# Norm 2 and the last step with a PSUM buffer per token tile, late-split columns, column sums by transposes, and buffers at multiples of 64 bytes

## The chip, the cores and the metric

The kernel runs on one core of a Trainium2 chip. The metric is device time in microseconds (us) of one execution; the median of several runs is quoted, and beside it one execution was recorded by the hardware profiler. Engines are named as the profile names them: PE is the matmul engine (TensorE), PEld its weight load, DVE is VectorE, ACT is ScalarE, POOL is GpSimd and SP is SyncE, which here issues nearly all transfers.

## The reference, cut to what matters

One layer of a diffusion backbone in fp32: 256 latent tokens of width 2048 (`x`), 256 context tokens, one conditioning vector `c` that yields six modulation vectors.

```python
mod = silu(c) @ w_mod + b_mod                      # (6 * 2048): sh1 sc1 g1 sh2 sc2 g2, segments 0 to 5
hx  = modulate(rms_norm(x, norm1_g), sh1, sc1)     # modulate(h, s, c) = h * (1 + c) + s
out = token_mixer(hx, ...)                         # two branches, gated and merged, then merged @ w_o
x   = x + g1 * out
h2  = modulate(rms_norm(x, norm2_g), sh2, sc2)     # "norm 2"
a, b = split(h2 @ w_up)                            # w_up: 2048 x 11264
a   = dwconv_grid(a, ffn_dw) + ffn_db              # 3 x 3 on a 4 x 64 grid
x   = x + g2 * ((silu(a) * b) @ w_down)            # w_down: 5632 x 2048
return rms_norm(x, final_g)
```

The change touches the segments 2 to 5 of `mod`, `merged @ w_o` with norm 2 behind it, the first columns of `h2 @ w_up`, and `@ w_down` with the last norm.

## The kernel before

**Products.** Every fp32 operand is split in two: a high half `hi` that is rounded to fp32r (ScalarE copy, L116) and a low half `lo`, the difference (VectorE subtraction, L117). A product is hi*hi + lo*hi + hi*lo. Weights come in blocks of 1 MB (`wload`, issued from SP, L78) into four buffers `raw`, and are split in halves of 1024 columns by `wsplit`: `w_hi` has five buffers, and the low halves lie first in the pool `lop` (five buffers on the right side of the memory), later in a ring `lo_ring` of one buffer `w_lo` (L659) and parts of the big activation tile `H` that are free by then (L634, L762), which is why a low half appears in the profile as `H`. The list `behind_of` says for the next splits on which engine the subtraction runs and after which instruction it is queued.

**Column blocks (`proj`).** The output is feature-major: 256 columns of a weight are two PSUM banks (a "bank pair", L57; three pairs exist). For each block of 8 k (k is a group of 128 rows), 16 wide matmuls of 128x512 take the high half of the weight times both halves of the activation, and 16 narrow ones of 128x256 the low half; `wide_next` swaps which of the two comes first from one block to the next. All matmuls are recorded at L135.

**Token products (`token_product`, `residual`).** `merged @ w_o` and `@ w_down` are token-major: four column blocks `cq` of 512, and for each two token tiles t of 128 tokens, six matmuls of 128x512 per k. `residual` multiplies by the broadcast gate `macc` (L830), adds to `x` (L831), sums squares on ScalarE (L833) and, at cq = 3, takes root (L837) and reciprocal (L838). At cq = 3 the second token tile is cut in two pieces of 256 columns (`pieces`) for every k, and the first piece shares a bank pair with token tile 0.

**Modulation beside the main work (`mod_steps`).** `pump` takes one step at a time, put between the other products: VectorE accumulates `silu(c)` times a row block of `w_mod` into `macc` (128 x 2048, cleared by a memset on POOL, L665, with the bias row behind it in POOL's queue). Segments 4 and 3, in this order, need their sum over the partitions as columns: `pc` (L672 to L679), 16 matmuls of one column with `macc` as weights. Segments 2 and 5 become rows broadcast to all partitions.

**Norm 2.** `x` is transposed by PE (`ptx`, L871), scaled by `g2c` into `xg`; the two reciprocals go on diagonals `dg` (L864, one buffer), whose product with ones, `rb`, spreads them over the partitions. Then a loop over eight pairs of k multiplies `xg` by `rb` (L886), adds `sh2` and rounds on ScalarE (the high half of h2) and subtracts on VectorE (L891, the low half); VectorE's order is written by hand there (`manual_schedule`). The first block of w_up follows with `proj` on two column blocks. Elsewhere a scheduler, which works from a model of the times, orders each engine's instructions.

**The end.** After cq = 3 of w_down the last norm scales `x` (ScalarE and VectorE) and SP issues eight stores (L970), four for each token tile.

Of the kernel before, what the change touches and what calls it, by code (L numbers as in the profile page):

```python
# [16 lines left out]
P = 128  # L17
T = 256
# [18 lines left out]
def hybrid_layer_kernel(ctx: ExitStack, tc: tile.TileContext, I, out, dbg=None):  # L37
# [19 lines left out]
    def bank_pair(name):  # L57

        return psW.tile([P, 2, 512], F32, name=name, tag="acw")
# [337 lines left out]
    def proj(w, cols, src, kt):  # L397
# [16 lines left out]
                wide_next[0] = not wide_next[0]  # L414
        return [acc[:].rearrange("p n (s t) -> p n s t", s=2) for acc in accs]

    def proj_xc(w, cols):
# [244 lines left out]
    def mod_steps():  # L662
        for seg in (4, 3, 2, 5):
            acc = map_.tile([P, D], F32, name="macc", tag="macc")
            nc.gpsimd.memset(acc[:], 0.0)  # L665
            nc.gpsimd.dma_start(acc[0:1, :], b_mod[0:1, seg * D:seg * D + D])
            for k in range(KD):
                raw = wload([(w_mod[k * P:k * P + P, seg * D:seg * D + D], (2048,))])
                nc.vector.scalar_tensor_tensor(out=acc[:], in0=raw[:], scalar=cst[:, k, 0:1], in1=acc[:], op0=ALU.mult, op1=ALU.add)  # L669
                if k < KD - 1:  # L670
                    yield
            if seg in (3, 4):  # L672
                pc = psH.tile([P, KD], F32, name="pc2", tag="psh")
                for k in range(KD):
                    mm(pc[:, k:k + 1], acc[:, k * P:k * P + P], ones[:, 0:1], k == 0, k == KD - 1)
                if seg == 3:
                    nc.vector.tensor_copy(sh2[:], pc[:])
                else:
                    nc.vector.scalar_tensor_tensor(out=g2c[:], in0=pc[:], scalar=1.0, in1=n2g, op0=ALU.add, op1=ALU.mult)  # L679
# [100 lines left out]
    def token_product(w, kt, cq, part, tail=1):  # L780


        accs = {}
        slots = [bank_pair("to")] + ([bank_pair("to")] if cq == 3 else [])
        slots = [pair[:, i] for pair in slots for i in range(2)]
        for t in range(2):
            for i, cs in enumerate(pieces(cq, t)):
                accs[t, i] = slots[t + i][:, :cs.stop - cs.start]

        def product(t, i, k, src, hv, lv):  # L790
            ts = slice(t * P, t * P + P)
            cs = pieces(cq, t)[i]
            mm(accs[t, i], src(k % 2, 0)[:, ts], hv[:, cs], k == 0, False)
            mm(accs[t, i], src(k % 2, 0)[:, ts], lv[:, cs], False, False)
            mm(accs[t, i], src(k % 2, 1)[:, ts], hv[:, cs], False, k == kt - 1)

        todo = []
        for c in range(kt // 4):
            for k4, hv, lv in wviews([wblock(w, c * 512, 4, cq * 512, 512)], 4):
                k = 4 * c + k4  # L800
                if k % 2 == 0:
                    src = part(k)
                todo.append((k, src, hv, lv))
            if c < kt // 4 - tail:
                for args in todo:
                    for t, i in accs:
                        product(t, i, *args)
                todo = []
        for t in range(2):
            own = range(len(pieces(cq, t)))  # L810
            for args in todo[:-4]:
                for i in own:
                    product(t, i, *args)
            for i in own:
                for args in todo[-4:]:
                    product(t, i, *args)
        return accs

    def pieces(cq, t):

        return (slice(0, 256), slice(256, 512)) if cq == 3 and t == 1 else (slice(0, 512),)

    def residual(accs, cq, bc, pool):

        for t in range(2):
            for i, cs in enumerate(pieces(cq, t)):
                n = cs.stop - cs.start
                xs = slice(cq * 512 + cs.start, cq * 512 + cs.stop)
                tt = pool.tile([P, 512], F32, name="res", tag="res", bufs=1)
                nc.vector.tensor_tensor(out=tt[:, :n], in0=accs[t, i], in1=bc[:, xs], op=ALU.mult)  # L830
                nc.vector.tensor_tensor(out=x1[:, t, xs], in0=x1[:, t, xs], in1=tt[:, :n], op=ALU.add)  # L831
                sq = pool.tile([P, 512], F32, name="sq", tag="sq", bufs=1)
                nc.scalar.activation(sq[:, :n], x1[:, t, xs], AF.Square, accum_out=ssq2[:, cq + i, t:t + 1])  # L833
            if cq == 3:
                if t == 1:
                    nc.vector.scalar_tensor_tensor(out=ssq2[:, 0, 1:2], in0=ssq2[:, 3, 1:2], scalar=1.0 / D, in1=ssq2[:, 0, 1:2], op0=ALU.mult, op1=ALU.add)
                root = nc.scalar.activation(r2[:, t:t + 1], ssq2[:, 3 + t, t:t + 1], AF.Sqrt, scale=1.0 / D, bias=ssq2[:, 0, t:t + 1])  # L837
                nc.vector.reciprocal(r2[:, t:t + 1], r2[:, t:t + 1])  # L838
        if cq in (1, 2):
            nc.vector.tensor_tensor(out=ssq2[:, 0, :], in0=ssq2[:, 0, :], in1=ssq2[:, cq, :], op=ALU.add)  # L840
        if cq == 2:
            nc.vector.tensor_scalar(out=ssq2[:, 0, :], in0=ssq2[:, 0, :], scalar1=1.0 / D, scalar2=EPS, op0=ALU.mult, op1=ALU.add)
        return root if cq == 3 else None

    def mg_part(k0):
        return lambda k, p: mg[:, k0 + k, p, :]
# [10 lines left out]
    for cq in range(4):  # L857
        accs = token_product(w_o, KD, cq, mg_part)
        norm2 = residual(accs, cq, bcast[2], tw)
        if cq == 3:  # L860
            rb = bank_pair("rb")[:, 0, 0:T]
            for t in range(2):
                dg = tw.tile([P, P], F32, name="dg", tag="dg", bufs=1)
                nc.vector.tensor_scalar(out=dg[:], in0=ident[:], scalar1=r2[:, t:t + 1], scalar2=None, op0=ALU.mult)  # L864
                mm(rb[:, t * P:t * P + P], ones, dg[:], t == 0, t == 1)
        for k2 in range(2):
# [13 lines left out]
    h2_hi = {}  # L880
    h2_lo = {}
    with tc.manual_schedule(engines={nc.vector.engine}):
        for k2 in range(KD // 2 + 1):
            if k2 < KD // 2:
                ks = slice(2 * k2, 2 * k2 + 2)
                nc.vector.tensor_tensor(out=xg[:, ks, :], in0=xg[:, ks, :], in1=rbv, op=ALU.mult)  # L886
                for k in range(2 * k2, 2 * k2 + 2):
                    h2_hi[k2] = nc.scalar.activation(hx[:, k, 1, :], xg[:, k, :], AF.Identity, bias=sh2[:, k:k + 1])
            if k2 > 0:
                for k in range(2 * k2 - 2, 2 * k2):  # L890
                    h2_lo[k2 - 1] = nc.vector.scalar_tensor_tensor(out=hx[:, k, 0, :], in0=xg[:, k, :], scalar=sh2[:, k:k + 1], in1=hx[:, k, 1, :].bitcast(F32),  # L891
                                                   op0=ALU.add, op1=ALU.subtract)
# [12 lines left out]
    w_up = I["w_up"][0]  # L905
    for j in range(NF // 2):
        cols = [256 * j, FF + 256 * j]
        pa_, pb_ = proj(w_up, cols, hx, KD) if j == 0 else proj(w_up, cols[:1], hx, KD) + [None]
# [51 lines left out]
    for t in range(2):  # L960
        for cq in (0, 1, 3, 2):
# [8 lines left out]
            nc.sync.dma_start(out[0, t * P:t * P + P, cs], v1)  # L970


_INS = ["x", "c", "ctx", "c_ctx", "w_mod", "b_mod", "norm1_g", "w_in", "lb_raw", "a_norm_g", "sconv_w",
# [29 lines left out]
```

## Time and profile before

| | |
|---|---|
| median of 3 runs | 1745.35 us (1743.7 to 1745.82) |
| profiled execution | 1744.56 us, its span 1742.6 us |
| PE busy | 1706.6 us, 98% of the span |
| VectorE, ScalarE, POOL busy | 76%, 52%, 1% |
| mean granted TensorE clock | 0.991 |
| DMA | 384.85 MB, mean 221 GB/s |

The span is the time from the first to the last recorded work of the profiled execution; 1.96 us of its 1744.56 lie around it. A row of a timeline gives start and length in us, the engine, the line, the operation, out<-in and shapes; in brackets stands the idle time of the engine just before, and what ended it. "128*128 128x512" is a weight tile of 128 by 128 with 512 columns that stream by. The granted clock (PEclk) is a share of full speed. In a row of groups stand the line, operation and shapes, then busy time and mean ns of one, then the idle time before.

### The profile page before, as it was taken

Reading aid. Unit: us, or ns where it says so; the run is one execution under the profiler, and the core shown is the slowest. Engines: PE = TensorE matmul, PEld = TensorE weight load, DVE = VectorE, ACT = ScalarE, POOL = GpSimd, SP = SyncE. Lnnn points to the kernel's source line nnn. Section 1 sums busy time; section 2 is a strip of 40 time slices with the busy share of each in tenths; the row PEclk is TensorE's granted clock in tenths of the full one; section 3 lists DMA queues with packets and bytes.
Section 4 is the critical chain, followed back from the end, with each engine's and each line's share of the span. In section 5 each row is a group of like instructions: output and inputs, shape, how many; then the busy total and the mean of one; then the engine's idle time right before and its main releaser. Section 6 shows DMA issues by size and latency. Waiting matters only on the chain.

```text
span 1742.6 us, 24110 instructions
## 1 busy us (share of the span) xinstructions
PE 1706.6 (98%) x9623; PEld 1443.0 (83%) x9623; DVE 1316.2 (76%) x1694; ACT 899.7 (52%) x1156; POOL 20.0 (1%) x25
## 2 busy tenths in 40 slices
PE   5999999999999999999999899999999999999997
PEld 3567878788888888898888788888888888888886
DVE  4447267668998978878865589888888877876774
ACT  5226246556655644544555454444555554765653
POOL 0000000000000000000000100000000000000000
PEclk9999999999999999999999899999999999999999
DMA  9996323224777778878976357776666755655552
GB/s 360 348 336 196 105 64 121 73 97 148 263 248 265 270 252 312 311 285 325 328 273 205 116 198 242 242 242 236 233 236 238 241 173 190 218 193 193 194 193 73
DMA packets 293045, 384.85 MB, mean 221 GB/s; under 512 B 7780, under 2 KB 245645, under 8 KB 284102
## 3 DMA queue, kind: packets, MB, share of 16 engines
q1 hardware_dynamic: 291968, 379.82, 63.7%
q10 hardware_dynamic: 694, 3.24, 0.5%
q8 instruction: 75, 1.23, 0.3%
q0 software_dynamic: 272, 0.26, 0.1%
q14 instruction: 36, 0.29, 0.1%
HBM read 381.20 MB, written 2.10 MB: 220 GB/s over the span
## 4 chain that ended last, share of the span: by engine, by line
PE 97%; DVE 1%; ACT 1%; issue 0%; DMA 0%; ACTq 0%; DVEq 0%
PE acc L135 56%; PE to L135 19%; PE acx L135 6%; PE vacc L135 5%; PE zacc L135 5%; PE pm L135 2%; PE ps L135 2%; PE po L135 1%; PE pc L135 0%; DMA rows_a<-in_norm_g_dram 0%; PE pt L247 0%; PE pm L324 0%; PE kdt L510 0%; ACT H L233 0%; DVE xt L240 0%
## 5 line engine op out<-in xcount | busy, mean ns | idle before, releaser
L116 ACT ACTIVATE w_hi<-raw 128x1024 fp32r<-128x1024 f32 x506 | 533.3, 1058 | 463.7 <-PE acc L135 334.3
L135 PE MATMUL acc<-H,w_hi 128*128 128x512 f32 x2688 | 636.6, 392 | 2.9 <-DVE H L891 2.3
L117 DVE TENSOR_TENSOR H<-raw,w_hi 128x1024 fp32r<-128x1024 f32 x427 | 517.9, 1221 | 133.1 <-ACT w_hi L116 124.4
L135 PEld LDWEIGHTS acc<-H,w_hi 128*128 128x128 f32 x2688 | 500.5, 189 | 104.3 <-DVE H L891 3.3
L135 PEld LDWEIGHTS acc<-H 128*128 128x128 f32 x2360 | 297.3, 192 | 7.4 <-DVE H L117 1.1
L135 PE MATMUL acc<-H 128*128 128x256 f32 x2360 | 303.1, 284 | 0.1
L135 PE MATMUL to<-w_hi,H 128*128 128x512 f32 (+1 forms) x792 | 221.4, 365 | 0.0
L669 DVE SCALAR_TENSOR_TENSOR macc<-raw,cst,macc 128x2048 f32<-128x2048 f32 x64 | 150.3, 2348 | 27.9 <-DMA raw<-in_w_mod_dram 24.0
L135 PEld LDWEIGHTS to<-w_hi,H 128*128 128x128 f32 x792 | 142.8, 188 | 24.3
L135 PE MATMUL to<-H 128*128 128x512 f32 (+1 forms) x396 | 144.9, 366 | 0.0
L117 DVE TENSOR_TENSOR w_lo<-raw,w_hi 128x1024 fp32r<-128x1024 f32 x78 | 94.8, 1221 | 62.0 <-ACT w_hi L116 53.3
L926 DVE SCALAR_TENSOR_TENSOR cvf<-av,pf,cvf 128x189 f32<-128x189 f32 (+2 forms) x352 | 130.3, 425 | 0.7 <-ACT cvf L914 0.7
L131 ACT ACTIVATE H<-y 128x512 fp32r<-128x512 f32 x88 | 55.1, 630 | 87.8 <-PE to L135 86.2
L135 PE MATMUL acx<-H,w_hi 128*128 128x512 f32 x288 | 93.3, 398 | 0.0
L132 DVE TENSOR_TENSOR H<-y,H 128x512 fp32r<-128x512 f32 x88 | 60.6, 690 | 36.8 <-ACT H L131 36.6
L135 PEld LDWEIGHTS to<-H 128*128 128x128 f32 x396 | 74.6, 188 | 12.2
L135 PE MATMUL vacc<-w_hi,H 128*128 128x512 f32 x256 | 82.2, 398 | 0.0
L135 PE MATMUL to<-w_hi,mg 128*128 128x512 f32 (+1 forms) x288 | 81.1, 367 | 0.0
L135 PE MATMUL zacc<-H,w_hi 128*128 128x512 f32 x224 | 78.1, 412 | 1.9 <-ACT H L335 1.9
L135 PEld LDWEIGHTS acx<-H,w_hi 128*128 128x128 f32 x288 | 53.6, 188 | 12.5
L135 PEld LDWEIGHTS zacc<-H,w_hi 128*128 128x128 f32 x224 | 42.0, 190 | 26.0 <-issue 10.9
L335 ACT ACTIVATE H<-xsT,md 128x256 fp32r<-128x256 f32 x32 | 16.7, 591 | 84.9 <-DVE md L329 84.9
(229 smaller groups left out, 1579.0 us busy)
## 6 DMA issues: line engine op xcount, KB each, us to landing
raw<-in_w_up_dram SPq DMA_DIRECT2D x88, 1024.0 KB, 4.9
raw<-in_w_in_dram SPq DMA_DIRECT2D x81, 1024.0 KB, 5.1
raw<-in_w_mod_dram SPq DMA_DIRECT2D x64, 1024.0 KB, 5.1
raw<-in_w_down_dram SPq DMA_DIRECT2D x44, 1024.0 KB, 5.0
raw<-in_w_mod_dram SPq DMA_DIRECT2D x64, 512.0 KB, 6.8
raw<-in_w_o_dram SPq DMA_DIRECT2D x16, 1024.0 KB, 5.0
raw<-in_w_in_dram SPq DMA_DIRECT2D x16, 512.0 KB, 3.8
raw<-in_w_pa_dram SPq DMA_DIRECT2D x8, 1024.0 KB, 5.3
```

The costliest lines, as they stand in the source:

```text
L116: nc.scalar.activation(hi, half, AF.Copy)
L117: sub.tensor_tensor(op=ALU.subtract, **operands)
L131: nc.scalar.activation(hi, src, AF.Copy)
L132: nc.vector.tensor_tensor(out=lo, in0=src, in1=hi.bitcast(F32), op=ALU.subtract)
L135: return nc.tensor.matmul(o, lhsT, rhs, start=start, stop=stop, skip_group_check=True)
L335: upper = nc.scalar.activation(H[:, kk, 1 + i, :], src, AF.Identity, scale=mv[:, 1, k, i:i + 1], bias=mv[:, 0, k, i:i + 1])
L669: nc.vector.scalar_tensor_tensor(out=acc[:], in0=raw[:], scalar=cst[:, k, 0:1], in1=acc[:], op0=ALU.mult, op1=ALU.add)
L926: nc.vector.scalar_tensor_tensor(out=c4[:, ro, co], in0=a4[:, ri, ci], scalar=pf[:, tap * NF + f:tap * NF + f + 1], in1=c4[:, ro, co], op0 ...
```

## The change

Eight edits, with L-numbers of before:

1. A tile of 32 bytes (`edge`) is put at the right edge of the memory, so that the pools on the right side (`lop`, `map`, `tp`, `xp`: w_lo, macc, z, x1 and others) begin at multiples of 64 bytes; before, they began 32 bytes off one.
2. Column sums of segments 4 and 3: 16 transposes by PE in four groups of 4, each group summed along its free axis by a TENSOR_REDUCE on VectorE.
3. `token_product` at cq = 3: a bank pair for each token tile, and a third bank (`rest`) for the last four k of the right 256 columns of tile 1; only these four k are cut in pieces of 256. `residual` does the 512 columns of tile 1 first, then `rest`. Root and reciprocal of tile 0 are queued ahead of the work on tile 1.
4. Two buffers for `dg`.
5. The first multiply of the h2 loop is cut in two of 256 columns, and the first pair of low halves comes ahead of the second multiply.
6. The first block of w_up goes by `proj_both`: both column blocks per 8 k, all wide matmuls ahead of all narrow ones.
7. The subtractions around the loop: the first three are free to run ahead of it, all on VectorE (before, one, on POOL); of those tied to the loop five are left. The memset of `macc` for segment 5 is queued after the last low half of h2.
8. The last of the eight stores is issued by ScalarE.

```diff
+    edge = ctx.enter_context(tc.tile_pool(name="edge", bufs=1, side="right"))
+    edge.tile([P, 8], F32, name="edge")
     lop_cm = tc.tile_pool(name="lop", bufs=5, side="right")
...
+    def proj_both(w, cols, src):
+        accs = [bank_pair("acc") for _ in cols]
+        for c in range(KD // 8):
+            both = zip(*[wsplit([wblock(w, c * 1024, 8, c0, 256)]) for c0 in cols])
+            parts = [(8 * c + 4 * i + k, k * 256, part) for i, part in enumerate(both) for k in range(4)]
+            for wide in (True, False):
+                for k, at, part in parts:
+                    for acc, p in zip(accs, part):
...
+        wide_next[0] = False
...
+                if seg == 5:
+                    behind.enter_context(tc.issue_after(h2_lo[KD // 2 - 1].ins))
+                nc.gpsimd.memset(acc[:], 0.0)
...
-                pc = psH.tile([P, KD], F32, name="pc2", tag="psh")
-                for k in range(KD):
-                    mm(pc[:, k:k + 1], acc[:, k * P:k * P + P], ones[:, 0:1], k == 0, k == KD - 1)
...
+                for k4 in range(KD // 4):
+                    pc = psH.tile([P, 4, P], F32, name="pc", tag="psh")
+                    for k in range(4):
+                        at = (4 * k4 + k) * P
+                        nc.tensor.transpose(pc[:, k, :], acc[:, at:at + P], ident[:])
+                    nc.vector.tensor_reduce(out=col[:, 4 * k4:4 * k4 + 4], in_=pc[:], op=ALU.add, axis=mybir.AxisListType.X)
...
+            accs = [bank_pair("to")[:, 0] for t in range(2)]
+            rest = bank_pair("to")[:, 0, 0:256]
...
+                for args in todo[-4:]:
+                    product(t, *args, cs=slice(0, 256))
+                for args in todo[-4:]:
+                    product(t, *args, acc=rest, cs=slice(256, 512))
...
-                dg = tw.tile([P, P], F32, name="dg", tag="dg", bufs=1)
+                dg = tw.tile([P, P], F32, name="dg", tag=f"dg{t}", bufs=1)
...
-    behind_of += [((), nc.gpsimd)] + [((h2_hi[i], h2_lo[i]), nc.vector) for i in range(7)]
+    behind_of += [((), nc.vector)] * 3 + [((h2_hi[i], h2_lo[i]), nc.vector) for i in (1, 3, 4, 5, 6)]
...
-            nc.sync.dma_start(out[0, t * P:t * P + P, cs], v1)
+            (nc.scalar if t == 1 and cq == 2 else nc.sync).dma_start(out[0, t * P:t * P + P, cs], v1)
```

How the instructions stand on PE around the first column sum (`pc`; `acc` are the column blocks of `proj`, `pt<-ident,rows_f` are transposes of the convolution's weights), before:

```order
L135 MATMUL acc<-H 128x256 x32
L135 MATMUL acc<-H,w_hi 128x512 x16
L135 MATMUL pc_4931<-ones_r,macc 128x1 x16
L135 MATMUL acc<-H,w_hi 128x512 x16
L135 MATMUL acc<-H,w_lo 128x256 x8
L740 MATMUL pt<-ident,rows_f 128x110 x3
L135 MATMUL acc<-H 128x256 x3
```

And after:

```order
L137 MATMUL acc<-H,w_hi 128x512 x16
L700 MATMUL pc<-ident,macc 128x128 x8
L137 MATMUL acc<-H,w_hi 128x512 x16
L137 MATMUL acc<-H,w_lo 128x256 x5
L700 MATMUL pc<-ident,macc 128x128 x4
L137 MATMUL acc<-H,w_lo 128x256 x2
L700 MATMUL pc<-ident,macc 128x128 x4
L137 MATMUL acc<-H,w_lo 128x256
L137 MATMUL acc<-H 128x256 x24
L137 MATMUL acc<-H,w_hi 128x512
L764 MATMUL pt<-ident,rows_f 128x110 x3
```

The 16 one-column matmuls in one place became 16 transposes in groups of 8, 4 and 4, with matmuls of the main work between them.

VectorE from the last products of w_o to the first pairs of h2 (`res` and `x` are the residual, `r` the reciprocal, `xg` the multiply by `rb`, `H<-xg,sh,H` the low halves of h2, `H<-raw,w_hi` low halves of weights), before:

```order
L117 TENSOR_TENSOR H<-raw,w_hi 128x2x512
L830 TENSOR_TENSOR res<-to,macc 128x512
L831 TENSOR_TENSOR x_7188<-x_7188,res 128x512
L830 TENSOR_TENSOR res<-to,macc 128x256
L831 TENSOR_TENSOR x_7188<-x_7188,res 128x256
L830 TENSOR_TENSOR res<-to,macc 128x256
L838 RECIPROCAL r_7190<-r_7190 128x1
L836 SCALAR_TENSOR_TENSOR ssq_7189<-ssq_7189 128x1
L831 TENSOR_TENSOR x_7188<-x_7188,res 128x256
L864 TENSOR_SCALAR dg<-ident,r_7190 128x128
L838 RECIPROCAL r_7190<-r_7190 128x1
L864 TENSOR_SCALAR dg<-ident,r_7190 128x128
```

And after:

```order
L119 TENSOR_TENSOR H<-raw,w_hi 128x2x512 x4
L853 TENSOR_TENSOR res<-to,macc 128x512
L854 TENSOR_TENSOR x_7205<-x_7205,res 128x512
L853 TENSOR_TENSOR res<-to,macc 128x512
L854 TENSOR_TENSOR x_7205<-x_7205,res 128x512
L863 RECIPROCAL r_7207<-r_7207 128x1
L853 TENSOR_TENSOR res<-to,macc 128x256
L907 TENSOR_SCALAR dg<-ident,r_7207 128x128
L883 SCALAR_TENSOR_TENSOR ssq_7206<-ssq_7206 128x1
L854 TENSOR_TENSOR x_7205<-x_7205,res 128x256
L863 RECIPROCAL r_7207<-r_7207 128x1
L907 TENSOR_SCALAR dg<-ident,r_7207 128x128
```

Four weight subtractions now stand right ahead of the first residual, where one stood, and the residual of tile 1 covers 512 columns and then 256.

VectorE in the h2 loop behind that, before:

```order
L886 TENSOR_TENSOR xg<-xg,rb 128x512 x2
L891 SCALAR_TENSOR_TENSOR H<-xg,sh_3465,H 128x256 x2
L886 TENSOR_TENSOR xg<-xg,rb 128x512
L117 TENSOR_TENSOR H<-raw,w_hi 128x2x512
L891 SCALAR_TENSOR_TENSOR H<-xg,sh_3465,H 128x256 x2
```

And after:

```order
L930 TENSOR_TENSOR xg<-xg,rb 128x256 x2
L938 SCALAR_TENSOR_TENSOR H<-xg,sh_3469,H 128x256 x2
L932 TENSOR_TENSOR xg<-xg,rb 128x512 x2
L938 SCALAR_TENSOR_TENSOR H<-xg,sh_3469,H 128x256 x2
L932 TENSOR_TENSOR xg<-xg,rb 128x512
L119 TENSOR_TENSOR H<-raw,w_hi 128x2x512
```

The second multiply moved behind the first low halves, and the first subtraction inside the loop one pair later.

More of the change, by code (lines that the diff above doesn't have):

```diff
@@ L664, in mod_steps @@
             acc = map_.tile([P, D], F32, name="macc", tag="macc")
-            nc.gpsimd.memset(acc[:], 0.0)
+            with ExitStack() as behind:
+                if seg == 5:
+                    behind.enter_context(tc.issue_after(h2_lo[KD // 2 - 1].ins))
+                nc.gpsimd.memset(acc[:], 0.0)
             nc.gpsimd.dma_start(acc[0:1, :], b_mod[0:1, seg * D:seg * D + D])
@@ L780, in token_product, with product @@
     def token_product(w, kt, cq, part, tail=1):
[L783 to L790, printed above, removed]
-            ts = slice(t * P, t * P + P)
[L792 to L795, printed above, removed]
+        if cq < 3:
+            pair = bank_pair("to")
+            accs = [pair[:, t] for t in range(2)]
+        else:
+            accs = [bank_pair("to")[:, 0] for t in range(2)]
+            rest = bank_pair("to")[:, 0, 0:256]
+        def product(t, k, src, hv, lv, acc=None, cs=slice(0, 512)):
+            ts = slice(t * P, t * P + P)
+            own = acc is not None
+            acc = acc if own else accs[t][:, cs]
+            mm(acc, src(k % 2, 0)[:, ts], hv[:, cs], k == (kt - 4 if own else 0), False)
+            mm(acc, src(k % 2, 0)[:, ts], lv[:, cs], False, False)
+            mm(acc, src(k % 2, 1)[:, ts], hv[:, cs], False, k == kt - 1)
         todo = []
@@ L805, in token_product @@
                 for args in todo:
-                    for t, i in accs:
-                        product(t, i, *args)
+                    for t in range(2):
+                        product(t, *args)
                 todo = []
         for t in range(2):
-            own = range(len(pieces(cq, t)))
             for args in todo[:-4]:
-                for i in own:
-                    product(t, i, *args)
-            for i in own:
+                product(t, *args)
+            if cq < 3 or t == 0:
@@ L815, in token_product @@
                 for args in todo[-4:]:
-                    product(t, i, *args)
-        return accs
-    def pieces(cq, t):
-        return (slice(0, 256), slice(256, 512)) if cq == 3 and t == 1 else (slice(0, 512),)
-    def residual(accs, cq, bc, pool):
[L825 to L843, printed above, removed]
@@ new lines, in token_product, with add_gated @@
+                    product(t, *args)
+            else:
+                for args in todo[-4:]:
+                    product(t, *args, cs=slice(0, 256))
+                for args in todo[-4:]:
+                    product(t, *args, acc=rest, cs=slice(256, 512))
+                accs.append(rest)
+        return accs
+    def add_gated(acc, t, c0, n, bc, pool):
+        xs = slice(c0, c0 + n)
+        tt = pool.tile([P, 512], F32, name="res", tag="res", bufs=1)
+        nc.vector.tensor_tensor(out=tt[:, :n], in0=acc, in1=bc[:, xs], op=ALU.mult)
+        nc.vector.tensor_tensor(out=x1[:, t, xs], in0=x1[:, t, xs], in1=tt[:, :n], op=ALU.add)
@@ L907, in hybrid_layer_kernel @@
         cols = [256 * j, FF + 256 * j]
[L908 removed]
+        pa_, pb_ = proj_both(w_up, cols, hx) if j == 0 else proj(w_up, cols[:1], hx, KD) + [None]
         av = tw.tile([P, 2, T], F32, name="av", tag="av")
```

67 lines of the change are left out of this document (54 added, 13 removed).

## The prediction

> **What bounds the kernel now.** I read the page first, then the chain of waits, then the granted TensorE clock in stretches, then the timeline of the four places that the change touches. Two lines of the page say nearly all:
>
> ```profile
> PE 1706.6 (98%) x9623; PEld 1443.0 (83%) x9623; DVE 1316.2 (76%) x1694; ACT 899.7 (52%) x1156; POOL 20.0 (1%) x25
> PE 97%; DVE 1%; ACT 1%; issue 0%; DMA 0%; ACTq 0%; DVEq 0%
> ```
>
> TensorE is the bound from some 35 us to the end. A change can help in three ways only: fewer microseconds of matmul, fewer stalls of PE (two are left: norm 2 and the last step), or a higher clock. The clock is in the windows (columns: length, busy time and count by engine, PEclk, DMA share, GB/s):
>
> ```profile
> 619.90:626.70 6.80, 6.80 (x23) 5.93 (x23) 2.99 (x5) 1.09 (x3) 4.32 (x5) 0.51 0.54 175
> 756.30:759.70 3.40, 3.40 (x18) 3.30 (x17) 0.00 (x0) 0.00 (x0) 2.14 (x2) 0.50 0.44 155
> 991.90:1002.10 10.20, 6.98 (x18) 4.58 (x18) 8.42 (x16) 8.47 (x17) 0.88 (x2) 0.50 0.26 87
> 1002.10:1008.50 6.40, 6.40 (x34) 5.35 (x34) 6.40 (x11) 4.76 (x9) 0.00 (x0) 1.00 0.59 193
> ```
>
> PE counts as busy in the first two, yet it runs at half clock, for 6.8 and 3.4 us; at norm 2 for 10.2 us. The first two follow the column sums, whose matmuls stream one column each: to the clock that is nearly idleness.
>
> **Column sums (L672 to L679).** The PE timeline (start, length, instruction):
>
> ```profile
> 602.90 7.43 PE L135 MATMUL acc<-H,w_hi 128*128 128x512 f32 x32
> 610.17 4.00 PE L135 MATMUL acc<-H 128*128 128x256 f32 x32
> 614.01 3.82 PE L135 MATMUL acc<-H,w_hi 128*128 128x512 f32 x16
> 617.67 4.88 PE L135 MATMUL pc<-ones_r,macc 128*128 128x1 f32 x32
> 622.41 5.88 PE L135 MATMUL acc<-H,w_hi 128*128 128x512 f32 x16
> 628.13 1.10 PE L135 MATMUL acc<-H,w_lo 128*128 128x256 f32 x8
> ```
>
> Start to start, a wide matmul takes (610.17 - 602.90)/32 = 0.227 us and a narrow one (614.01 - 610.17)/32 = 0.120. The first sum holds PE from 617.67 to 622.41, 4.74 us, and the 16 wide ones behind it take 5.72 where 3.64 is normal: 2.08 lost to the clock. The second sum:
>
> ```profile
> 752.46 3.63 PE L135 MATMUL pc<-ones_r,macc 128*128 128x1 f32 x32
> 755.94 3.46 PE L135 MATMUL acc<-H 128*128 128x256 f32 x16
> 759.20 1.11 PE L135 MATMUL acc<-H,w_hi 128*128 128x512 f32 x3
> ```
>
> It takes 3.48, and 16 narrow ones then take 3.26 for 1.92: 1.34 lost, and some 0.25 more up to 759.7. In their place come 16 transposes a sum, in groups of 8, 4 and 4 with product matmuls between. The nearest rows are eight transposes of the earlier stage, from the chain in order of time, and the clock around them:
>
> ```profile
> 206.45 0.87 PE kdt L510 x8
> 200.00:240.00 40.00, 40.00 (x275) 1.00 0.25 80
> ```
>
> 0.109 us each, 1.74 a sum, no drop. Gain: 4.74 + 2.08 - 1.74 = 5.08, and 3.48 + 1.59 - 1.74 = 3.33, together **8.4**. VectorE gets eight TENSOR_REDUCEs of 512 PSUM elements for two small operations; bounds 0.19 (the reduce of 32 elements) and 0.69 (a 512-element read of PSUM, row 987.53 below). I take 0.69, since the length sets the time: 2.8 a sum, costed at nothing on PE:
>
> ```profile
> L326 DVE TENSOR_REDUCE md<-pm 128x8 f32<-128x32 f32 x7 | 1.3, 191 | 5.2 <-PE pm L324 5.2
> 632.00:700.00 68.00, 68.00 (x394) 60.21 (x393) 60.18 (x51) 33.06 (x38) 0.00 (x0) 1.00 0.94 335
> ```
>
> VectorE has 7.8 of 68 us free behind the first sum. The third group of transposes needs the first reduce done (two PSUM buffers), but stands behind 16 wide and 5 narrow matmuls, 4.2 us. The rows_f transposes move up as well; their loads are queued on POOL behind VectorE's L724 and have some 3 us to land. I cost both at nothing.
>
> [...]
>
> **The split last columns (token_product).** At cq = 3 the second token tile was split into 256-wide pieces for every k; now only for the last four. Two rows of the last step inside cq = 3, one k apart:
>
> ```profile
> 1671.85 0.40 PE L135 MATMUL to<-H 128*128 128x512 f32 x1
> 1673.25 0.40 PE L135 MATMUL to<-H 128*128 128x512 f32 x1
> ```
>
> With its split half a k takes 1673.25 - 1671.85 = 1.40; six wide matmuls, as now, are 6 x 0.227 = 1.36. So 0.04 per k: **0.5** for 12 k of w_o and **1.6** for 40 k of w_down.
>
> **Norm 2.** VectorE between the last products of w_o and the first matmul of w_up, and three rows of PE:
>
> ```profile
> 987.53 0.69 DVE L830 TENSOR_TENSOR res<-to,macc 128x512 f32<-128x512 f32 x1 [10.74 <-PE to L135]
> 990.60 0.42 DVE L831 TENSOR_TENSOR x<-x,res 128x256 f32<-128x256 f32 x1
> 990.93 1.40 DVE L864 TENSOR_SCALAR dg<-ident,r 128x128 f32<-128x128 f32 x1
> 991.98 0.36 DVE L838 RECIPROCAL r<-r 128x1 f32<-128x1 f32 x1
> 993.23 0.29 DVE L864 TENSOR_SCALAR dg<-ident,r 128x128 f32<-128x128 f32 x1 [0.89 <-PE rb L135]
> 994.40 1.28 DVE L886 TENSOR_TENSOR xg<-xg,rb 128x512 f32<-128x512 f32 x2 [0.89 <-PE rb L135]
> 995.67 0.88 DVE L891 SCALAR_TENSOR_TENSOR H<-xg,sh,H 128x256 fp32r<-128x256 f32 x2
> 988.65 0.28 PE L135 MATMUL to<-w_hi,mg 128*128 128x256 f32 x1
> 996.21 2.08 PE L135 MATMUL acc<-H,w_hi 128*128 128x512 f32 x4 [1.84 <-DVE H L891]
> 1008.55 2.08 PE L135 MATMUL acc<-H 128*128 128x256 f32 x16
> ```
>
> The last product ends at E = 988.93. Token tile 0 was complete 24 narrow matmuls earlier, at E - 2.88, but its residual started at E - 1.40, with the first piece of tile 1: both lie in one PSUM pair. With a pair each it starts at E - 2.83. Then, back to back on VectorE: two operations of 0.69 to E - 1.42; two on the 512 columns of tile 1 (but for the last four k of the right 256, which the third bank holds) to E + 0.02; reciprocal 0.17 (row 1735.89 below); that rest 0.42; dg 0.29; the sum of squares, one column like the reciprocal, 0.17; x 0.42, with small gaps to E + 1.6. From the end of x to the start of the second reciprocal lay 991.98 - 991.02 = 0.96, as after. Reciprocal 0.17 (0.36 was beside the memset of macc on POOL, as was the dg of 1.40, which now wait for the last h2); dg 0.29; it no longer waits for the first rb product, having a buffer of its own. That is E + 3.0. From the end of dg to xg lay 994.40 - 993.52 = 0.88. A 256-wide multiply for 0.42, the 256-wide ACT step and one VectorE step at about 0.45 each (half of row 995.67), and 0.13 for gaps: first matmul at E + 5.35 instead of E + 7.28, **1.9** earlier.
>
> From 996.21 to 1008.55 PE ran 30 wide and 16 narrow matmuls: 8.7 us of work in 12.3, 3.6 lost, to half clock and because VectorE took 2.5 us per pair of h2 blocks (multiply 0.68, two lowers 0.88, one weight subtraction between). Three subtractions now run before, and PE does both column blocks of w_up for each pair, 8 wide = 1.8 us. My schedule of VectorE gives pairs at 0, 2.2, 4.9 and 6.5 us after PE's start; at full clock that loses 1.3, at half clock for the first 4.6 us 2.3. PE is still without products for 5.4 us, longer than one step of the clock (3.4), so it drops; I take 2.0: **1.6** more. Norm 2 gives 3.5; bounds 1.5 and 4.3.
>
> **The end.**
>
> ```profile
> 1730.83 0.69 DVE L830 TENSOR_TENSOR res<-to,macc 128x512 f32<-128x512 f32 x1 [10.28 <-PE to L135]
> 1731.94 0.28 PE L135 MATMUL to<-w_hi,H 128*128 128x256 f32 x1
> 1735.89 0.17 DVE L838 RECIPROCAL r<-r 128x1 f32<-128x1 f32 x1 [0.58 <-ACT r L837]
> 1734.54 4.49 SPq L970 DMA_DIRECT2D out_dram<-x  x8
> ```
>
> PE ends at F = 1732.22, the span at F + 10.38. Tile 0 waits here too, until 1730.83; it could start at F - 5.6, and its residual, root and four stores are then over before F. What stays is tile 1: rest and x to F + 0.95, square, root and reciprocal to F + 2.1 instead of F + 3.84. The eight stores took 4.49 us of SP's queue, one after the other, the last begun at F + 6.25 and 4.1 before the end. Now SP has three left and ACT issues the fourth: the last begins at F + 3.6, the end at F + 7.7. Gain **2.6**; bounds 1.7 (the reciprocal alone) and 3.6 (stores that also land sooner).
>
> **Buffers at multiples of 64 bytes.** The right-hand buffers (w_lo, z, macc, x1) were 32 bytes off and are not now.
>
> ```profile
> L147 DVE TENSOR_TENSOR z<-acc,z 128x512 f32<-128x512 f32 x28 | 19.2, 685 | 0.5
> L147 DVE TENSOR_TENSOR av<-acc,av 128x512 f32<-128x512 f32 x22 | 15.2, 691 | 1.3 <-ACT av L146 0.2
> L135 PEld LDWEIGHTS acc<-H,w_lo 128*128 128x128 f32 x328 | 41.6, 188 | 1.0
> L135 PEld LDWEIGHTS acc<-H 128*128 128x128 f32 x2360 | 297.3, 192 | 7.4 <-DVE H L117 1.1
> 162.08 44.37 PE vacc L135 x192
> ```
>
> z and w_lo lay off, av and H did not: 685 against 691, 188 against 192. I take 0. One row leaves room: vacc runs at 44.37/192 = 0.231 against 0.227; were all of that the address, the 1152 matmuls of the stages zacc, acx and vacc would gain 4.5; were the 192 the price of a multiple, 352 loads of w_lo would lose 1.4. [...]
>
> **Sum.** 8.4 + 0.5 + 3.5 + 1.6 + 2.6 = 16.6 off the profiled 1744.56 (span 1742.6): 1727.9. The median of the three, 1745.35, is 0.8 above the profiled execution: **1728.7**.
>
> **Rivals.**
> 1. The forecast, 0.62.
> 2. Transposes drop the clock as the one-column matmuls did, for one step of 3.4 us a sum, at half speed: 3.4 more, 1732.1. [...] 0.12.
> 3. The stretch behind the sums is bound by transfers: 335 GB/s and a DMA share of 0.94 in 632 to 700. PE then waits for raw, and the 8.4 are given back: 1737.1. Against it: PE is busy for all 68 us there. 0.12.
> 4. The change does not do at norm 2 what it says: one of the subtractions now queued ahead of the residual on VectorE waits for a w_hi buffer that only the last product frees, and all behind it with it. The 3.5 are lost: 1732.2. 0.05.
> 5. The addresses give 4.5 more: 1724.2. 0.06.
> 6. Slower: VectorE becomes the bound behind the sums. Its reduces stand at the head of its queue until PE reaches the later groups: 4.2 us at the first sum and, behind 16 narrow and 16 wide, 5.5 at the second, with eight reduces of 0.69 on top: 15.2, and the 8.4 gone: 1728.7 + 23.6 = 1752.3. It decides from where that exceeds VectorE's free time, 7.8 of 68 us. Against it: VectorE's idle time is on both sides of the sums, and weights are split several halves ahead. 0.03.
>
> The range reaches from 1722 (norm 2 and the end at their best with some of rival 5) to 1736.5, just short of rival 3; it leaves out 0.15 above. About 0.2% (3.5 us) can be told from no change here: faster 0.95, same 0.02, slower 0.03.
>
> **What would show it.** Right: the clock stays at 1.00 through both sums, and 16 transposes start 0.11 apart; the residual of tile 0 starts 2.8 before the last product of w_o ends; no dg over 0.3; first w_up matmul 5.4 after; PE's last matmul to the span's end 7.7. Wrong: a wait of PE for raw or for a w_lo behind 630, a third TENSOR_REDUCE with idle time of microseconds, or half clock after a sum.

## The result, and the profile after

The changed kernel takes 1727.36 us (median of 4 runs, 1725.19 to 1728.24) against 1745.4 before: ratio 0.9900, 95% interval [0.9888, 0.9912], 18 us or 1% less. The profiled execution took 1726.84, its span 1725.1. The page of the changed kernel, and from its windows the stretch of both column sums (columns as in the prediction):

```profile
PE 1693.0 (98%) x9435; PEld 1425.7 (83%) x9435; DVE 1325.5 (77%) x1703; ACT 907.2 (53%) x1156; POOL 17.7 (1%) x24
```

```profile
600.00:780.00 180.00, 180.00 (x1054) 159.40 (x1053) 154.25 (x141) 85.01 (x100) 6.63 (x7) 1.00 0.85 301
```

PE is the bound as before, with 13.6 us less of busy time, and the clock is full through both sums. In the PE timeline of the changed kernel the first sum looks like this, with the y_a matmul that stood at 636.01 before; the last two rows stand around the second sum:

```profile
617.83 1.04 PE L700 MATMUL pc<-ident,macc 128*128 128x128 f32 x8
618.63 3.88 PE L137 MATMUL acc<-H,w_hi 128*128 128x512 f32 x16
622.35 0.75 PE L137 MATMUL acc<-H,w_lo 128*128 128x256 f32 x5
622.94 0.60 PE L700 MATMUL pc<-ident,macc 128*128 128x128 f32 x4
623.62 0.60 PE L700 MATMUL pc<-ident,macc 128*128 128x128 f32 x4
631.17 3.79 PE L137 MATMUL acc<-y_a,w_hi 128*128 128x512 f32 x16
746.54 1.07 PE L137 MATMUL acc<-H,w_lo 128*128 128x256 f32 x8
765.91 3.79 PE L137 MATMUL acc<-y_a,w_hi 128*128 128x512 f32 x16
```

The 16 wide matmuls behind the first group take 622.35 - 618.63 = 3.72 us where they took 5.72. (In the rows of before, each of the 16 one-column matmuls counts as two instructions, hence x32.) Norm 2 in the changed kernel, from the timelines of VectorE, POOL and PE, and one of its windows:

```profile
977.10 0.69 DVE L853 TENSOR_TENSOR res<-to,macc 128x512 f32<-128x512 f32 x1 [0.40 <-PE to L137]
980.55 0.29 DVE L907 TENSOR_SCALAR dg<-ident,r 128x128 f32<-128x128 f32 x1
982.40 0.29 DVE L907 TENSOR_SCALAR dg<-ident,r 128x128 f32<-128x128 f32 x1
983.27 0.75 DVE L930 TENSOR_TENSOR xg<-xg,rb 128x256 f32<-128x256 f32 x2 [0.58 <-PE rb L137]
980.68 1.90 POOL L687 MEMSET macc<- 128x2048 f32 x1 [222.38 <-ACT sq L858]
979.65 0.28 PE L137 MATMUL to<-w_hi,mg 128*128 128x256 f32 x1
984.90 8.84 PE L137 MATMUL acc<-H,w_hi 128*128 128x512 f32 x32 [1.67 <-DVE H L938]
```

```profile
985.00:990.00 5.00, 5.00 (x17) 4.03 (x18) 5.00 (x10) 4.21 (x8) 0.00 (x0) 0.73 0.01 3
```

The residual of tile 0 starts 2.83 us before the last product ends (979.93), no dg takes over 0.29, and the first w_up matmul comes 4.97 behind that end. One step of half clock is left: it ends at 987.7, 2.8 us behind the first w_up matmul. The end:

```profile
1711.43 0.69 DVE L853 TENSOR_TENSOR res<-to,macc 128x512 f32<-128x512 f32 x1 [5.84 <-PE to L137]
1714.68 6.36 SPq L1025 DMA_DIRECT2D out_dram<-x  x7
1716.70 0.28 PE L137 MATMUL to<-w_hi,H 128*128 128x256 f32 x1
```

The stores of tile 0 begin at 1714.68, before PE ends at 1716.98; the span ends 8.1 us later instead of 10.4.

Where the 17.5 us of the span came from, by the starts of the same matmul in both PE timelines (step: how much later or earlier it comes in the changed kernel than at the mark above it):

| mark | before | changed | step |
|---|---|---|---|
| first vacc | 161.92 | 163.25 | +1.33 |
| 16 wide ahead of the first sum | 614.01 | 614.17 | -1.17 |
| first y_a behind it | 636.01 | 631.17 | -5.00 |
| 8 narrow ahead of the second sum | 751.52 | 746.54 | -0.14 |
| first y_a behind it | 774.21 | 765.91 | -3.32 |
| first of w_o | 897.17 | 888.68 | -0.19 |
| last of w_o | 988.65 | 979.65 | -0.51 |
| first of w_up | 996.21 | 984.90 | -2.31 |
| first of w_down | 1490.70 | 1477.28 | -2.11 |
| last of w_down | 1731.94 | 1716.70 | -1.82 |
| end of span | 1742.6 | 1725.1 | -2.3 |

Two things were in no term of the sum: +1.33 ahead of vacc, and the 1.5 of the rows where no instruction of PE differs (-1.17, -0.14, -0.19).

### The profile page after: what moved, and what is told of

The parts are those of the page before. It is cut to its first block, busy times and chain, and to the rows that moved or that the text cites. A ratio compares the mean times of both kernels' runs of the same rounds, so it can differ in the third digit from the quotient of the medians.

```text
span 1725.1 us, 23733 instructions
## 1 busy us (share of the span) xinstructions
PE 1693.0 (98%) x9435; PEld 1425.7 (83%) x9435; DVE 1325.5 (77%) x1703; ACT 907.2 (53%) x1156; POOL 17.7 (1%) x24
## 4 chain that ended last, share of the span: by engine, by line
PE 97%; ACT 1%; DVE 1%; issue 0%; DMA 0%; ACTq 0%; DVEq 0%
PE acc L137 57%; PE to L137 19%; PE acx L137 6%; PE vacc L137 5%; PE zacc L137 5%; PE pm L137 2%; PE ps L137 2%; PE po L137 1%; DMA rows_a<-in_norm_g_dram 0%; PE pt L249 0%; PE pm L326 0%; PE kdt L529 0%; PE pc L700 0%; ACT H L235 0%; DVE x L854 0%
## 5 line engine op out<-in xcount | busy, mean ns | idle before, releaser
L137 PE MATMUL to<-w_hi,H 128*128 128x512 f32 (+1 forms) x712 | 217.1, 387 | 0.0
L137 PEld LDWEIGHTS to<-w_hi,H 128*128 128x128 f32 x712 | 133.2, 188 | 27.1
L981 DVE SCALAR_TENSOR_TENSOR cvf<-av,pf,cvf 128x189 f32<-128x189 f32 (+2 forms) x352 | 134.7, 429 | 13.2 <-ACT cvf L969 12.7
L137 PE MATMUL to<-H 128*128 128x512 f32 (+1 forms) x356 | 137.6, 387 | 0.0
L137 PEld LDWEIGHTS to<-H 128*128 128x128 f32 x356 | 66.9, 188 | 13.7
```

Of the source, the lines that this page charges most:

```text
L137: return nc.tensor.matmul(o, lhsT, rhs, start=start, stop=stop, skip_group_check=True)
L981: nc.vector.scalar_tensor_tensor(out=c4[:, ro, co], in0=a4[:, ri, ci], scalar=pf[:, tap * NF + f:tap * NF + f + 1], in1=c4[:, ro, co], op0 ...
```

## The experiments

Each kernel's median is given with the ratio to the kernel before and its interval. The kernel before was timed anew beside each group of experiments, and its own median was 1745.4 beside the changed kernel, then 1745.11 (experiments 1 to 4), 1744.59 (5, 7, 10 and the first of 9) and 1743.75 (6, 8, 11 and the second of 9). So medians of different groups are up to 1.7 us apart without any edit, and the number of half-clock steps varies by itself (below). A term is therefore read from the marks of the profiled executions.

**1 and 2. The address alone.** The edge tile added to the kernel before, and taken out of the changed one:

```diff
+    edge = ctx.enter_context(tc.tile_pool(name="edge", bufs=1, side="right"))
+    edge.tile([P, 8], F32, name="edge")
```

> The kernel before with the 32-byte edge tile alone. As I predicted (address worth nothing): 1745.4, and the 192 matmuls of the first vacc stage take 44.4 us as in the kernel before. Rival from the two traces (the stage lost 1.03 us between the vacc rows, and narrow matmuls with w_lo as weights went from 0.117 to 0.114 us): 1.0 to 1.5 us faster, 1743.9 to 1744.4, vacc 43.97. The earlier rival of 4.5 us, an address price on every matmul of the stages zacc, acx and vacc: 1740.9.

> The changed kernel without the edge tile, all else as changed. Address worth nothing: 1727.4. Rival: 1.0 to 1.5 us slower, 1728.4 to 1728.9, first vacc stage back to 44.4 us for 192 matmuls.

Measured: 1742.29 (0.9987 [0.9978, 0.9995]) with the tile on before; 1727.53 without it in the changed kernel, against 1727.36. The chain of waits has the first vacc stage with the tile on before:

```profile
162.70 43.97 PE vacc L137 x192
```

and without it in the changed kernel:

```profile
162.12 44.38 PE vacc L135 x192
```

The tile decides it in both kernels. From the first vacc to the first matmul of w_o, leaving out the two sums, before with the tile is 1.5 us shorter than before, and the changed kernel without it has none of the 1.5. So the address is worth 1.5 us: a gain that I had put at 0. The medians differ by 2.8 (1742.29 against 1745.11); in the profiles the rest is clock, since that run had one half-clock step at the first sum where the profiled before had two. That the two medians of the changed kernel agree can be chance of the same kind: its profile without the tile has one such step at the start of the program, the one with it two.

**3. The column sums alone**, L672 to L679 of the diff on the kernel before.

> The kernel before with the column sums by transposes and nothing else. Theory (16 one-column matmuls cost their own time plus a step of half clock behind them): 8.3 us faster, 1737.1, clock 1.00 from 600 to 780 us. Rival (the gain of the changed kernel is there only together with its other edits, since PE then waits for weights behind the sums): less than 4 us faster, with a wait of PE for raw or for a low half behind 630 us.

Measured: 1737.58 (0.9961 [0.9948, 0.9973]).

```profile
600.00:780.00 180.00, 180.00 (x1055) 159.55 (x1054) 153.68 (x141) 84.88 (x101) 6.64 (x7) 1.00 0.84 298
```

Between the marks the sums gain 5.03 and 3.27, as in the changed kernel (5.00 and 3.32), and PE does not wait: theory holds, the rival falls. The median is 7.5 lower and not 8.3; the profile had more half clock at the start and behind norm 2 than that of before.

**4. Do transposes count as work to the clock?**

```diff
-                    for k in range(4):
+                    for k in list(range(4)) * 8:
```

> The changed kernel with each of its column-sum transposes made eight times over (same result), so that 64 stand in a row, 7.0 us, twice as long as a step of the clock. Theory (transposes count as work to the clock): 0.109 us each, 2 x 112 x 0.109 = 24.4 us slower, 1751.8, clock 1.00 at both sums. Rival (they do not count): at least one step of half clock at each sum, two for the first 64, and 1.7 to 7 us more at each, 1755 to 1766.

Measured: 1752.5 (one run).

```profile
617.79 14.14 PE L700 MATMUL pc<-ident,macc 128*128 128x128 f32 x128
```

```profile
617.00:630.00 13.00, 13.00 (x117) 12.79 (x116) 7.17 (x9) 2.92 (x5) 1.99 (x3) 1.00 0.33 107
```

All 128 of the first sum stand in a row: PE did nothing but transposes for 14 us, four steps of the clock, at clock 1.00, and each cost 0.109. They kept the clock up; the rival falls. Whether transposes would raise it from half, no run here shows.

**5. The PSUM pair.**

```diff
-            accs = [bank_pair("to")[:, 0] for t in range(2)]
+            pair = bank_pair("to")
+            accs = [pair[:, t] for t in range(2)]
```

> The changed kernel with both token tiles of cq = 3 in one PSUM bank pair again (the late split and its own bank for the rest stay). Theory (the residual of tile 0 waits for tile 1 when they share a pair): it starts 1.4 us before the end of the last product of w_o instead of 2.8, first w_up matmul 1.4 later, at 6.4 us instead of 5.0 behind that end; at the end of the kernel the four stores of tile 0 come 4 us later but the last store no more than 1.4; in all 2 to 3 us slower, 1729.4 to 1730.4. Rival (the pair is not what it waits for): 1727.4 and no change of the residual's start.

Measured: 1729.76 (0.9915 [0.9899, 0.9932]). VectorE at norm 2 (two rows) and at the end, and SP's queue:

```profile
977.09 0.69 DVE L854 TENSOR_TENSOR res<-to,macc 128x512 f32<-128x512 f32 x1 [1.83 <-PE to L137]
983.42 0.75 DVE L931 TENSOR_TENSOR xg<-xg,rb 128x256 f32<-128x256 f32 x2 [0.89 <-PE rb L137]
1716.06 0.69 DVE L854 TENSOR_TENSOR res<-to,macc 128x512 f32<-128x512 f32 x1 [10.00 <-PE to L137]
1719.88 4.04 SPq L1026 DMA_DIRECT2D out_dram<-x  x7
```

The residual of tile 0 starts 1.4 us before the last product ends, as forecast: it is the pair that it waits for. The first w_up matmul comes 6.56 behind that end, 1.6 more. Of this 1.3 is the pair, for the second dg starts that much later; 0.3 is the clock, at half in this run when rb was made, so that xg waited 0.89 and not 0.58. The span ends 10.6 behind PE (2.5 more, where I had said no more than 1.4): the four stores of tile 0 then stand ahead of those of tile 1. The profiled span is 3.0 longer in all, since this run had one half-clock step less at the start.

**6. The last store.** All eight on SP again.

> The changed kernel with all eight stores issued by SP. If the store on ScalarE's queue carries part of the 2.3 us gained at the end: the span ends 8.4 us or more behind PE's last matmul instead of 8.07, 1727.8. If the pair of its own for each token tile carries all of it (the shared pair alone cost 2.5 us there): within 0.15 us of 8.07, 1727.4.

```profile
1715.70 6.86 SPq L1025 DMA_DIRECT2D out_dram<-x  x8
```

The end comes 8.17 behind PE's last matmul, against 8.07: the store on ScalarE's queue is worth 0.1, the pair nearly all the rest. (Median 1728.07, 0.9909 [0.9894, 0.9923]; the profiled run had two half-clock steps at norm 2.)

**7 and 8. The first block of w_up, and the weight subtractions.**

```diff
-        pa_, pb_ = proj_both(w_up, cols, hx) if j == 0 else ...
+        pa_, pb_ = proj(w_up, cols, hx, KD) if j == 0 else ...
```

> The changed kernel with the first block of w_up by proj as before (one column block after the other, wide and narrow in turn), all else as changed. Theory (both column blocks per pair of h2 give PE 1.8 us of work per pair instead of 0.9): from the first w_up matmul on, 1.5 to 2.2 us of the loss come back, 1729 to 1729.6, with PE waiting for low halves of h2. Rival (the loss was the half clock alone, and the subtractions moved ahead did the rest): within 0.5 us of 1727.4.

```diff
-    behind_of += [((), nc.vector)] * 3 + [((h2_hi[i], h2_lo[i]), nc.vector) for i in (1, 3, 4, 5, 6)]
+    behind_of += [((), nc.gpsimd)] + [((h2_hi[i], h2_lo[i]), nc.vector) for i in range(7)]
```

> The changed kernel with the list of weight subtractions as before: one on POOL, seven tied to the pairs of h2, none on VectorE ahead of the residual but the one that stood there. Theory (a subtraction inside the loop holds VectorE 1.2 us and PE behind it): the first 128 w_up matmuls take 0.8 to 2.4 us longer than the changed kernel's 23.65, 1728.2 to 1729.8. Rival (PE has enough work from two column blocks per pair): within 0.3 us, 1727.4.

Measured: 1727.14 (0.9898 [0.9883, 0.9912]) and 1727.84 (0.9908 [0.9893, 0.9923]): the rival both times, but not by the medians. The old block had no half clock behind norm 2, and beside the kernel with the memset made twice, which had none either, its w_up takes 0.4 longer (table below), not 1.5 to 2.2. With the old subtractions the first 128 w_up matmuls take 25.00 us, 1.35 more than the 23.65 of the changed kernel and so within the forecast, yet PE waits for nothing among them: the run had two half-clock steps, and kernels with two take 25.07 (stores on SP) and 25.19 (memset free). So these 1.35 are the clock. With the old block PE does wait for a low half of a weight, at full clock, as the window behind the row shows:

```profile
988.03 1.19 PE L137 MATMUL acc<-H 128*128 128x256 f32 x8 [0.92 <-DVE H L119]
```

```profile
980.00:995.00 15.00, 11.41 (x60) 9.09 (x61) 13.18 (x26) 12.81 (x26) 2.01 (x2) 1.00 0.22 73
```

**9. The memset of macc.** Its order behind the last low half of h2 taken away, and, in another kernel, the memset made twice.

```diff
-                if seg == 5:
-                    behind.enter_context(tc.issue_after(h2_lo[KD // 2 - 1].ins))
```

> The changed kernel without the order that puts the memset of macc for segment 5 behind the last low half of h2. Theory (the memset on POOL slows VectorE's work on the diagonals while it runs): the second dg takes 1.4 us instead of 0.29 and the second reciprocal 0.36 instead of 0.16, the first w_up matmul comes 1.1 to 1.3 us later, 1728.5 to 1728.7. Rival (dg was slow for another reason, its single buffer): dg 0.29, 1727.4.

Measured: 1728.06 (0.9902 [0.9887, 0.9917]). POOL, and VectorE's second dg:

```profile
980.56 1.90 POOL L686 MEMSET macc<- 128x2048 f32 x1 [222.38 <-ACT sq L857]
982.29 0.29 DVE L906 TENSOR_SCALAR dg<-ident,r 128x128 f32<-128x128 f32 x1
```

```profile
985.00:990.00 5.00, 5.00 (x12) 3.88 (x13) 5.00 (x10) 4.33 (x8) 0.00 (x0) 0.50 0.03 6
```

The memset starts where it started with the order, 0.12 us behind the start of the first dg, and the first w_up matmul 4.96 behind the last product: that order does nothing here. The 1.5 us that it lost in w_up are a second half-clock step (PEclk 0.50 in the last row, 0.73 in the changed kernel).

```diff
                 nc.gpsimd.memset(acc[:], 0.0)
+                if seg == 5:
+                    nc.gpsimd.memset(acc[:], 0.0)
```

> The changed kernel with the memset of macc for segment 5 made twice, so that POOL is at it from about 980.7 to 984.5 and the second dg (at 982.4) falls into it. Theory (a dg that starts while the memset runs ends only with it; in the changed kernel the first dg starts 0.13 us ahead of the memset and the second as it ends): the second dg takes some 2.1 us instead of 0.29, the first w_up matmul comes 6.8 us behind the last product of w_o instead of 5.0, 1.8 us slower, 1729.2. Rival (the 1.40 us of before came of the single dg buffer or of the order on VectorE): dg 0.29, 1727.4.

```profile
979.59 1.90 POOL L687 MEMSET macc<- 128x2048 f32 x1 [222.38 <-ACT sq L860]
981.55 1.80 POOL L689 MEMSET macc<- 128x2048 f32 x1
981.32 0.29 DVE L909 TENSOR_SCALAR dg<-ident,r 128x128 f32<-128x128 f32 x1
```

My expectation missed: dg 0.29, 1725.33 (0.9897 [0.9880, 0.9913]). But the run did not make the collision either: the second dg started 0.17 before the first memset's end and 0.23 before the second began. It tells nothing apart.

**10. The clock at norm 2.** Ten matmuls of ones, their result never used, in PE's idle time.

```diff
+        for behind, n in zip(rb_mm, (4, 6)):
+            with tc.issue_after(behind.ins):
+                for _ in range(n):
+                    mm(accs[0][:, 0], ones_r[:], idle, True, True)
```

> The changed kernel with ten matmuls of ones (result never used) in PE's idle time at norm 2, four ahead of the second rb product and six behind it. Theory (PE's idleness there drops the clock for one step of 3.4 us): clock 1.00 through norm 2, the first 32 wide and 32 narrow w_up matmuls take 11.1 to 11.5 us instead of 12.5, 1.0 to 1.4 us faster than the changed kernel, 1726.0 to 1726.4. Rival (VectorE's low halves of h2 set the pace there, whatever the clock): clock 1.00 and the same time within 0.3 us, PE waiting for H instead.

Measured: 1725.9 (0.9890 [0.9876, 0.9905]).

```profile
980.00:995.00 15.00, 13.87 (x69) 10.75 (x69) 13.18 (x28) 12.41 (x27) 2.39 (x2) 1.00 0.25 82
```

```profile
984.29 4.18 PE L137 MATMUL acc<-H,w_hi 128*128 128x512 f32 x16 [0.20 <-DVE H L944]
988.88 3.93 PE L137 MATMUL acc<-H,w_hi 128*128 128x512 f32 x16 [0.41 <-DVE H L944]
```

The clock stays at 1.00, and PE now waits for VectorE's low halves. At norm 2 and in w_up the gain is only 0.4 beside the profiled changed kernel with its one step, nearly as the rival had it; beside runs with two steps it is 1.9.

**11. The clock at both places.** Sixteen more such matmuls in PE's two idle stretches ahead of the first zacc matmul:

```diff
+        if b == 0:
+            for _ in range(9):
+                fill(spare)
         for s in range(2):
...
+        if b == 0:
+            for _ in range(7):
+                fill(spare)
```

> The changed kernel with the ten matmuls of ones at norm 2 and 16 more in PE's two idle stretches ahead of the first zacc matmul (9 ahead of the transposes of the first block, 7 behind them; never used). Theory (idle stretches of 2.4 and 1.9 us there cost one or two steps of half clock, 3.4 us each): clock 1.00 from 20 us to the end of PE's work, the first 60 zacc matmuls are through 21.0 us after the first instead of 22.3 (one step) or 23.6 (two), 1723.5 to 1725. Rival (transfers or VectorE set the pace of that stage whatever the clock): the clock stays, the time is that of the kernel with ten, 1725.9.

Measured: 1724.07 (0.9887 [0.9872, 0.9901]), the lowest of all, though the interval overlaps that of the changed kernel. Its four runs lie within 0.17 us (1723.97 to 1724.14) where those of the changed kernel span 3.05. The start of both programs, the changed kernel's first:

```profile
25.00:45.00 20.00, 15.44 (x91) 8.10 (x81) 11.00 (x21) 8.18 (x13) 0.00 (x0) 0.83 1.07 377
```

```profile
25.00:45.00 20.00, 19.32 (x118) 11.85 (x111) 11.06 (x21) 8.19 (x13) 0.00 (x0) 1.00 1.07 387
```

The first vacc matmul comes at 160.97 instead of 163.25, though the transfers were as full in both (DMA share 1.07): theory holds. The other profiles agree: with one half-clock step at the start the first vacc matmul comes at 161.8 to 162.5, with two at 162.5 to 163.3. The profiled span is 2.7 shorter than that of the changed kernel, 2.3 of it here and 0.4 at norm 2 and in w_up.

**What the loop of norm 2 costs**, from all profiles: the time from the first w_up matmul to the first of w_down, by how long the clock was at half behind the first.

| kernel | at half clock, us | w_up, us |
|---|---|---|
| memset twice; ten of ones; both places | 0 | 491.96; 492.05; 492.06 |
| old first block | 0 | 492.39 |
| changed | 2.8 | 492.38 |
| no edge; shared pair | 3.4; 3.5 | 492.64; 492.71 |
| old subtractions | 5.3 | 493.73 |
| stores on SP; transposes eight times; memset free | 5.8; 5.9; 6.1 | 493.80; 493.83; 493.92 |
| before; edge on before; column sums on before | 5.9; 6.2; 8.3 | 494.49; 494.53; 495.49 |

At equal clock (5.9) the edits to the loop, the first block and the subtractions are worth 494.49 - 493.83 = 0.66 together, `proj_both` 0.3 to 0.4 of it. The other 1.45 of the 2.11 is one step of the clock.

## Why the prediction was right

It lay 1.3 us above the result, with every term of the right sign and the address missing. Luck had a part in the closeness: the 1.5 of the address, left out, and the 1.3 that the clock took at the start nearly cancel.

- **Column sums, 8.4: measured 8.3** (5.00 and 3.32). The step named (one-column matmuls are idleness to the clock, transposes are not) was shown twice, in experiments 3 and 4: clock 1.00 through the transposes, where before had 0.51 and 0.50 behind the sums. The reduces took 0.68 to 0.69 as taken, and PE waited for none.
- **Late split, 0.5 and 1.6: measured 0.5 and 1.8.**
- **Norm 2, 3.5: measured 2.3 + 2.1 = 4.4.** The first part was taken 0.4 too small, 0.3 of it since rb came at full clock: 0.58 from dg to xg, not 0.88. Of the 2.3, 1.3 is the pair and 0.3 this clock (experiment 5). The step that failed is "which now wait for the last h2": the memset of macc ran at 980.68, beside norm 2 as before. That dg nevertheless took 0.29 may come of its starting 0.13 us ahead of the memset; no run tests it. The second part, 1.6 for fewer half-clock steps and more work per pair, came near the measured 2.1 by luck: 1.45 is a step of the clock that came in some runs and not in others, and only 0.66 the order. What it was worked out from, that a gap longer than one step drops the clock, does not always hold: the old first block and the memset made twice had gaps of 4.97 us and kept it at 1.00.
- **The end, 2.6: measured 2.3.** The mechanism was the pair. What I priced beside it, a shorter queue on SP, is worth 0.1 (experiment 6): the last store began at F + 3.6 as worked out, but 4.5 us passed from there, not the 4.1 of the row of before.
- **Addresses, 0: measured 1.5.** The row that I dismissed, vacc at 0.231 a matmul, held the price: half of its excess over 0.227 went with the address, 44.37 to 43.97 for 192. I had both the row and the rival, and took 0.
- **The start of the program, not in the sum: +1.3**, since the profiled changed kernel had two half-clock steps at 35 us where before had one. With 1.5 for the address the sum would be 18.1, and the measured 17.5 would be 18.8 without these 1.3.
- Of the rivals, the second (clock) fell by experiments 3 and 4. Transfers: 0.93 DMA share and 336 GB/s in 630 to 690, no wait of PE. VectorE as the bound behind the sums: PE had no wait there either. The fourth did not occur: the subtractions ahead of the residual ended at 976.71, before it could start at 977.10. The fifth had the sign right and the size three times too large.

Still open: why the dg of before took 1.40. In three kernels, before and the two built on it, it ended 0.08 to 0.09 us behind the memset's end; in before, where it ran to 990.93 + 1.40 = 992.33:

```profile
990.45 1.80 POOL L665 MEMSET macc<- 128x2048 f32 x1 [9.20 <-DVE res L830]
```

In six of the other kernels (changed, no edge, ten of ones, memset free, memset twice, old subtractions) the memset begins while the first dg runs, 0.14 to 0.17 us before its end, and ends 1.73 to 1.74 behind that end; it takes 1.88 to 1.91 there, and the dg 0.28 to 0.29. The second dg of the changed kernel starts 0.18 before the recorded end of the memset and takes 0.29. How the memset and the dg are coupled, if they are, is not shown: the runs of experiment 9 did not settle it, and the single dg buffer of before was not tried by itself.

## What to carry to other kernels

Look for short matmuls and gaps of PE at which the granted clock falls: beside the time that they hold PE one pays for the slow work behind them (2.08 us behind the first sum). Transposes in their place, or matmuls of ones in the gap, kept the clock here (1.00 in 600 to 780 and in 980 to 995). Two residuals that were to start apart needed PSUM tiles of their own: in one pair that of tile 0 started 1.4 us before the end of the last product, with a pair each 2.83. Where a step of the clock comes in one run and not in the next, compare marks between stages and not medians: an edit worth 1.5 us showed as 2.8 in one pair of medians and as 0.2 in another.

## What the runs showed of the hardware

- **The clock fell in steps of 3.41 us whose phase was not the program's.** Up to PE's last matmul it was at half in the kernel before from 36.12 to 39.53, 619.80 to 626.62, 756.33 to 759.74 and 991.85 to 1002.09 us, in the changed kernel from 35.40 to 42.23 and 984.31 to 987.72: one to three steps at a time, and in each of the two traces all these changes lie whole multiples of 3.413 us apart. At the start both programs run within 0.1 us of each other (the last transposes ahead of the first zacc matmul at 34.04 and 34.08), yet the clock fell 0.72 apart. At norm 2 three kernels with nearly the same gap, not filled, had no step (old first block, 4.97 us), one (changed, 4.97) and two (memset free, 4.96). With the gaps at the start and at norm 2 filled, four runs lay within 0.17 us.
- **Reading w_lo at 32 bytes off a multiple of 64 cost PE some 1%**: 192 matmuls, of which every third streams w_lo, in 44.38 against 43.97 us, with nothing changed but the edge tile. Of the tiles that PE reads there, w_lo alone moved. VectorE did not feel it: z, which moved likewise, took 0.685 us before, 0.685 with the tile on before and 0.688 after.
- **The instruction order between engines was no wait here.** The memset ordered behind an instruction of VectorE ran 20 us ahead of it (980.68 against the last low half at 1000.89), and without the order it ran in the same place (experiment 9).
